# A list schedule that counts transfers by packets, the sample's bias copies moved to the prompt's attention, and four buffers for the u loads

## The chip, the cores and the metric

The kernel runs on one core of a Trainium2 chip. TensorE (PE) multiplies matrices; VectorE (DVE), ScalarE (ACT) and GpSimd (POOL) work elementwise and on rows; SyncE (SP) issues all transfers here, in the order of its queue (rows of SP in the profile are written SPq). Each engine works through its own instructions in their order, and waits where an operand is not there. The metric is the device time of one launch in microseconds, as the median of several runs.

## The reference

One encoder layer is applied with the same weights to a prompt of 512 tokens and a sample of 1024 tokens, each of width 1024:

```
h    = rmsnorm(x)
q_a,k_a,v_a,z_a, q_b,k_b,v_b,z_b, g_a,g_b = split(h @ w_in)
o_a  = neighbourhood_attention(rms(q_a), rms(k_a), v_a, rpb)   # 8 heads, 2-D window, bias
o_b  = window_gqa(rms(q_b), rms(k_b), v_b, t5 bias, sink)      # 8 heads, band of 3 blocks
A    = (o_a * silu(z_a)) @ w_o_a
B    = (o_b * silu(z_b)) @ w_o_b
y    = x + (sigmoid(g_a) * A + sigmoid(g_b) * B) @ w_out
```

All of it is float32. The kernel keeps that accuracy by splitting each operand into a high and a low part (`whi`/`wlo`, `hh`/`hl`, `fh`/`fl`) and adding three products, so one product is three matmuls (L1286, L1287, L1288 in the dense part, and L761 three times in the projections).

## The kernel before, in words

The program does four phases in turn: the prompt's attention (to about 200 us of the profile), the prompt's dense phase (gates z and g, output projections, `w_out`; from 222 to 405 us TensorE does nothing but this work), the sample's attention (405 to about 790 us) and the sample's dense phase (to the end).

Nobody writes the engines' order by hand. The kernel describes operations with `f.op` and `f.dma`: a choice of engines with an assumed duration each, a priority, what buffers it takes new, uses, or waits for. `Flow.run` then plays a simulation: at each moment it gives each engine the ready operation of the best priority whose buffers are free, adds the assumed duration, and emits the instruction. The order in which instructions were emitted is the order in which each engine does them on the chip. So an assumed duration is never waited for on the chip; it only decides what stands ahead of what. A transfer occupies the simulated SP for its issue time; its length is put on one simulated transfer resource (`dma_free`), and its data counts as landed 950 ns after that.

An attention phase goes in groups of heads. `att_weights` loads weights `w` (384 KB each, two buffers) with SP, ScalarE copies the high part `whi` (L602), POOL or VectorE subtracts for `wlo` (L607); projections (L761) into `p`; squares and row sums, POOL's `rs_v` (L792) and `rs_r` (L799) give the norm's factor, VectorE scales `qk` (L816), TensorE transposes it (L861) and ScalarE and VectorE copy `kt`, `qt`. Scores (L934), maximum, exps (L978, ScalarE), the reciprocal `rs` (L1002), the scaling `sb` (L1010), TensorE's transposes of `sb` (L1026), copies `pp` (L1032), the product with `v` (L1063), and the outputs `ot` to memory (`o_d`). Parts of the dense gates' work (matmuls L1286 to L1288 into bank `d`, with weights `fr` split into `fh` and `fl`) are put between as filling. `rstd` loads a tile of the sample (`xt`, 512 KB) and squares it (`junk`, L460) for the sample's norm during the prompt's attention.

The bias of the neighbourhood attention is prepared in memory: `expand` copies each head's table twice, shifted, into `rpb_x` (16 copies from memory to memory of 8 x 8 runs of 384 floats for each of prompt and sample), `raw` loads it (L682, L708), and POOL or VectorE adds the mask into `bias` (L695). For the sample the 16 copies are issued in the prompt's dense phase, released by the attention's last exps.

In the sample's dense phase the gated outputs `u` are kept in memory (`u_d`). For each of 8 blocks of columns and each half of the tokens, one `u` half (256 KB) is loaded into an `ot` buffer (two of them, L1552), split into `T` by ScalarE (L1168) and VectorE or POOL (L1173), and multiplied with `w_out`'s split weights. `post_z` (around L1417) multiplies an attention output with silu(z), for branch B through a strided view.

Of the kernel before, what the change touches and what calls it, by code (L numbers as in the profile page):

```python
# [10 lines left out]
F32 = mybir.dt.float32  # L11
F32R = mybir.dt.float32r
AF = mybir.ActivationFunctionType
ALU = mybir.AluOpType
# [26 lines left out]
P = 128  # L41
# [5 lines left out]
NT_P, NT_S = 512, 1024  # L47
# [93 lines left out]
class Flow:  # L141
# [43 lines left out]
        self.ops.append(o)  # L185
        return o

    def dma(self, emit, nbytes, prio, **kw):
        return self.op((("sp", 470),), lambda e: emit(), prio, lag=nbytes / 360, **kw)

    def stage(self, prio, close=(), open=(), make=()):

# [14 lines left out]
    def run(self):  # L207
# [58 lines left out]
        now, done, dma_free = 0, 0, 0  # L266
        while done < len(self.ops):
            for e in ready:
                while free_at[e] <= now:
                    skipped, got = [], None  # L270
                    while ready[e]:
                        item = heapq.heappop(ready[e])
                        o = item[2]
                        if o.eng is not None:
                            continue
                        ns = dict(o.choice)[e]
                        if all(room(v, n) for v, n in o.new) and not any(locked(v, e) or v.held and not v.t for v in o.vals) and not barred(o, e) and all(
                            e2 == e or backlog(e2, item) + n2 >= now + ns - BIAS.get((e, e2), 0) for e2, n2 in o.choice
                        ):
                            got = o  # L280
                            break
                        skipped.append(item)
                    for item in skipped:
                        heapq.heappush(ready[e], item)
                    if got is None:
                        break
                    got.eng = e
                    if got.port and e in ("dve", "pool"):
                        port = (e, now + ns)
                    for v, _ in got.new:  # L290
                        rota.setdefault(v.key, []).append(v)
                        v.make()
                    for v in got.vals:
                        v.lock = (e, now + ns)
                    got.emit(e)
                    free_at[e] = now + ns
                    at(now + ns, 0, got)
                    if got.lag:
                        dma_free = max(dma_free, now + ns + 650) + got.lag
                        at(dma_free + 950, 2, got)  # L300
            if not events:
                if DEBUG:
                    for e in ready:
                        for p, k, o in sorted(ready[e])[:4]:
                            print(e, p, k, [(v.tag, room(v, n), v.turn, len(rota.get(v.key, ()))) for v, n in o.new], [v.tag for v in o.vals])
                raise RuntimeError("no operation can go on")
            now = events[0][0]
            while events and events[0][0] == now:
                _, _, kind, o = heapq.heappop(events)
                if kind == 1:  # L310
                    o.left -= 1
                    if not o.left:
                        push(o)
                    continue
                if kind == 4:
                    continue
                if kind == 3:
                    o.free = True
                    continue
                if kind == 0 and o.lag:  # L320
                    continue
                done += 1
                for v in o.vals:
                    v.left -= 1
                    if not v.left:
                        at(now + self.LAG.get((o.eng, v.first), 100), 3, v)
                for x in o.outs:
                    lags = [self.LAG.get((o.eng, e), 100) for e, _ in x.choice]
                    at(now + min(lags), 1, x)
# [25 lines left out]
def encoder_kernel(  # L355
# [93 lines left out]
    def rstd(pool, x, t, prio, load_prio, bufs, after=(), load_after=(), out=None):  # L449

        val = lambda shape, dt, tag, n: f.value(pool, shape, dt, tag, n)
        xt = val([P, D], F32, "xt", bufs)
        junk = val([P, D], mybir.dt.bfloat16, "junk", 1)
        ss, v = (val([P, 1], F32, "n" + n, bufs) for n in "sv")
        r = out or val([P, 1], F32, "nr", bufs)
        rv = lambda: r.t[:, t : t + 1] if out else r.t
        f.dma(lambda: nc.sync.dma_start(xt.t, x[t * P : (t + 1) * P, :]), 524288, load_prio, new=[xt], after=load_after)
        f.op(
            (("act", ACT_(D) + 93),),
            lambda e: act.activation(junk.t, xt.t, AF.Square, accum_out=ss.t), prio, new=[junk, ss], use=[xt], after=after,  # L460
        )
        f.op(
            (("pool", 164),),
            lambda e: nc.gpsimd.tensor_scalar(v.t, ss.t, 1.0 / D, EPS, op0=ALU.mult, op1=ALU.add),
            prio, new=[v], use=[ss],
        )
        f.op(
            (("pool", 464),), lambda e: nc.gpsimd.tensor_tensor(rv(), v.t, mhalf[:, :1], op=ALU.pow),
            prio, use=[v], **({"into": [r]} if out and t else {"new": [r]}),
        )  # L470
        return xt, r
# [78 lines left out]
    def norm_tile_t(pool, x_t, rb, hh, hl, t, prio, load_prio):  # L550

        tok = slice(t * P, (t + 1) * P)
        xt = f.value(pool, [P, D], F32, "xt", 2)
        f.dma(
            lambda: nc.sync.dma_start(
                xt.t.rearrange("p (k n) -> p k n", n=P), x_t[:, :, tok].rearrange("k p n -> p k n")
            ),
            524288, load_prio, new=[xt],
        )
        src = lambda k: ([], lambda: xt.t[:, k * P : (k + 1) * P])  # L560
        return xt, scaled_parts(xt, src, lambda: rb.t[:, tok], rb, hh, hl, t, 4, prio)

    def norm_pair(pool, x_t, rb, hh, hl, t, t_d, prio, load_prio):
# [10 lines left out]
        for j, in0, in1, dst in (  # L574
# [12 lines left out]
                    t_d[j, :, :, t * P : (t + 1) * P].rearrange("k p n -> p k n"),  # L587
                    h[dst]().rearrange("p (k n) -> p k n", n=P),
                ),
                262144, prio, after=[o], hold=[(x0, x1)[dst[1]]],  # L590
            )
        return {t: sum(e0, ()), t + n: sum(e1, ())}, stores

    def att_weights(src, n, prio, engs=("pool", "dve"), place=None, after=()):
# [2 lines left out]
        hi = f.value(wpool, [P, 768], F32R, "whi", 6)  # L597
        lo = f.value(wpool, [P, 768], F32R, "wlo", 6)
        sv = lambda: st.t[:, at : at + n]
        ld = f.dma(lambda: nc.sync.dma_start(sv(), src), 512 * n, prio, after=after, **({"new": [st]} if new else {"hold": [st]}))  # L600
        a = f.op(
            (("act", ACT_(n) + 40),), lambda e: act.activation(hi.t[:, :n], sv(), AF.Copy),  # L602
            prio, new=[hi], hold=[st], after=[ld],
# [10 lines left out]
    def expand_ops(geo, prios, after):  # L614
        for h in range(8):
            expanded[geo.nt, h] = [
                f.dma(lambda h=h, lo=lo: expand(geo, h, lo), 196608, prios[h], after=after[h // 2]) for lo in range(2)
            ]

    def setup(pool, prio, after):  # L620
# [27 lines left out]
    def attention_phase(geo, hh, hl, h_ops, mask_d, early, late):  # L648
# [24 lines left out]
        def tables(br, g, prio):  # L673
            nb_t = tile_([P, max(2 * at[-1], 4 * GW)], F32, "bias", 2)
            first = [nb_t]
            for i in range(2 if br == "A" else 4):
                raw = tile_([P, max(GW, 48 * geo.cw)], F32, "raw", RAW[nt])
                if br == "A":
# [1 line left out]
                    h = 2 * g + i  # L680
                    sp(
                        lambda raw=raw, h=h: nc.sync.dma_start(raw.t[:, :run], rpb_x[nt][h]),  # L682
                        run * 512, prio, new=[raw], after=expanded[nt, h],
                    )
                    for o, n, c0 in [(a + o, n, c0) for a, (_, runs) in zip(at, a_tables) for o, n, c0 in runs]:
                        nw = n // P * cw
# [15 lines left out]
                else:  # L702
# [6 lines left out]

                    for lo in range(2):  # L710
                        kw = {"new": [raw], "after": line_op} if lo == 0 else {"into": [raw]}
                        sp(lambda raw=raw, h=h, lo=lo: emit_load(raw, h, lo), 98304, prio, **kw)

                    def emit(e, i=i, raw=raw):
                        ov = nb_t.t[:, i * GW : (i + 1) * GW].rearrange("p (w c l) -> p w c l", w=3, l=2)
# [242 lines left out]
        def weigh(br, gi, g, block, sums, pss, sbs, nb_t, info, prio):  # L958
# [114 lines left out]
            if br == "A":  # L1073
# [16 lines left out]
                        dst = over(o_d[nt][0, g, 64 * i : 64 * i + 64], runs)  # L1090
                        nc.sync.dma_start(dst, ot.t[:64, 2 * i].rearrange("p (a b) -> p a b", b=64))

                stores[g, runs[0][0] // 512].append(sp(emit, 65536, prio, use=[ot]))
            else:
                for e in range(2):
                    dst = o_d[nt][e, 4 + 2 * g : 6 + 2 * g, :, runs[0][0] : runs[0][0] + P]
                    dst = dst.rearrange("c (i d) n -> d (c i) n", d=64)
                    o = sp(
                        lambda e=e, dst=dst: nc.sync.dma_start(dst, ot.t[e * 64 : e * 64 + 64]),
                        131072, prio, use=[ot],  # L1100
                    )
                    for c in (4 + 2 * g, 5 + 2 * g):
                        for n in range(nt // 512):
# [32 lines left out]
    def dense_phase(geo, hh, hl, h_ops, o_stores, exps_done, start, opened, tp, up, p0, p1, p2, x_t, y_t, classic, fill, after_gates=None, side=None):  # L1136
# [269 lines left out]
        def post_z(c, a, n, v, in_psum, prio):  # L1406
# [3 lines left out]
            for e, ot in enumerate(ots):  # L1410
                if c < 4:
                    src, dst = o_d[nt][e, c, :, a : a + n], lambda ot=ot: ot.t[:, :n]
                else:
                    src = o_d[nt][e, c].rearrange("p (i n) -> p i n", n=P)[:, :, a // nb : a // nb + m]
                    dst = lambda ot=ot: ot.t[:, :n].rearrange("p (i n) -> p i n", n=m)
                dma(
                    lambda dst=dst, src=src: nc.sync.dma_start(dst(), src), 512 * n, prio - 0.5, new=[ot],  # L1417
                    after=o_stores[c, a // nh],
                )
            ot, ov, sv = ots[0], lambda: ots[0].t[:, :n], lambda: sg.t[:, :n]  # L1420
            if len(ots) > 1:
# [1 line left out]
            if c < 4:  # L1423
                tt(sv, sv, ov, ALU.mult, n, prio, use=[sg, ot], into=[sg])
            else:
                gv = lambda: sv().rearrange("p (n i) -> p n i", n=m)
                tt(gv, gv, lambda: ov().rearrange("p (i n) -> p n i", n=m), ALU.mult, n, prio, use=[sg, ot], into=[sg])
            if short:
                split_u(c, a, n, sg, prio)
            else:  # L1430
# [116 lines left out]
        if not short:  # L1547
            for c in range(8):
                for n in halves:
                    st = tile_("ot", n_ot)  # L1550
                    dma(
                        lambda st=st, c=c, n=n: nc.sync.dma_start(st.t, u_d[c, :, half[n]]), 512 * nh, 10 + c // 4,  # L1552
                        new=[st], after=stores["u", c, n],
# [105 lines left out]
    setup(norm_p, -0.7, h_ops["p"][1][:1])  # L1659
    expand_ops(gp, [max(-1, (h // 2 - 1) * gp.nb) for h in range(8)], [h_ops["p"][t][:1] for t in (1, 3, 3, 3)])  # L1660
    o_p, exps, start = attention_phase(gp, *h_p, h_ops["p"], mask_p, early["p"], late["p"])
    rb = f.value(rb_pool, [P, NT_S], F32, "rb", 1)
    r_s = f.value(norm_p, [P, gs.nb], F32, "r_s", 1)
    for t in range(gs.nb):
# [20 lines left out]
            h_ops["s"].update(ends)  # L1685
            t_stores.append(stores)

    expand_ops(gs, [4 + h for h in range(8)], [[exps]] * 4)
    dense_phase(
        gp, *h_p, h_ops["p"], o_p, exps, start, opened, t_pool["p"], u_pool, d0["p"], d1["p"], d2["p"], xt_p, y_p, CLASSIC_P,  # L1690
        FILL_P, None, norm_sample,
# [95 lines left out]
```

## Time and profile before

| | |
|---|---|
| runs (us) | 1142.96, 1141.8, 1140.71; median 1141.8 |
| profiled execution | 1145.24 us, of which the span from first to last instruction is 1143.4 us |
| busy: PE, DVE, ACT, POOL | 1129.6, 858.3, 645.1, 319.4 us |
| granted TensorE clock, mean | 0.998 |
| packets moved | 129314, 168.26 MB |

Busy is what an engine spent in instructions, issue and waiting not counted. Engines overlap, so the columns are not added. A wait in brackets at a row's end is the idle time ahead of it and what ended it. In the chain of work each piece is followed back from the last instruction to what released it; a transfer there runs from its issue to its landing. The windows give what each engine was busy within a stretch of the span.

### The profile page before, as it was taken

How to read it: one execution, taken by the hardware profiler on the slowest of the kernel's cores; microseconds unless marked ns; L12 is line 12 of the kernel's file. 1: busy time of each engine (PE TensorE's matmuls, PEld its weight loads, DVE VectorE, ACT ScalarE, POOL GpSimd, SP SyncE). 2: the span in 40 equal slices, each digit the busy share in tenths (PEclk: the TensorE clock that was granted, in tenths of full speed). 3: DMA queues.
4: the chain of work that ended last, by engine and by line, in shares of the span. 5: the costliest groups of instructions: out<-in, count | busy, mean ns of one | idle time of the engine just before them, and what ended most of it. 6: DMA issues, size and time to landing. Idle time of an engine off the chain costs nothing.

```text
span 1143.4 us, 18577 instructions
## 1 busy us (share of the span) xinstructions
PE 1129.6 (99%) x6115; PEld 981.9 (86%) x6115; DVE 858.3 (75%) x1994; ACT 645.1 (56%) x1477; POOL 319.4 (28%) x420
## 2 busy tenths in 40 slices
PE   8999999999999999999999999999999999999998
PEld 7989988888888889999899988888888888788887
DVE  6868797587766467887868888886878665497984
ACT  6767997544433246574659888875633334342320
POOL 4644443000010044443514343420123221032110
PEclk9999999999999999999999999999999999999999
DMA  7844643488797422121313214135767545564072
GB/s 267 275 140 129 189 118 97 106 257 256 237 277 210 157 91 72 29 79 29 91 31 93 72 38 121 46 111 160 262 179 228 194 161 186 196 230 130 28 221 93
DMA packets 129314, 168.26 MB, mean 147 GB/s; under 512 B 28809, under 2 KB 67473, under 8 KB 129218
## 3 DMA queue, kind: packets, MB, share of 16 engines
q1 hardware_dynamic: 129218, 167.08, 47.9%
q8 instruction: 48, 0.79, 0.3%
q14 instruction: 48, 0.39, 0.1%
HBM read 128.22 MB, written 43.54 MB: 150 GB/s over the span
## 4 chain that ended last, share of the span: by engine, by line
PE 92%; DMA 3%; DVE 2%; ACT 1%; POOL 1%; issue 1%; SPq 0%; POOLq 0%; DVEq 0%; ACTq 0%
PE p L761 23%; PE x L1288 10%; PE x L1287 10%; PE x L1286 10%; PE x L1063 5%; PE x L1026 5%; PE x L934 5%; PE p L1287 4%; PE p L1286 4%; PE p L1288 4%; PE d L1286 4%; PE d L1288 4%; PE d L1287 4%; PE x L861 2%; DMA w<-in_w_att_dram 1%
## 5 line engine op out<-in xcount | busy, mean ns | idle before, releaser
L761 PE MATMUL p<-whi,hh 128*128 128x384 f32 x384 | 133.8, 349 | 0.0
L761 PE MATMUL p<-whi,hl 128*128 128x384 f32 x384 | 132.7, 345 | 0.0
L761 PE MATMUL p<-wlo,hh 128*128 128x384 f32 x384 | 132.3, 345 | 0.0
L978 ACT ACTIVATE sb<-sb,mx 128x384 f32<-128x384 f32 (+1 forms) x192 | 107.8, 566 | 24.1 <-DVE mx L969 23.7
L761 PE MATMUL p<-whi,hb 128*128 128x384 f32 x384 | 107.8, 346 | 0.0
L1168 ACT ACTIVATE whi<-raw 128x512 fp32r<-128x512 f32 (+1 forms) x124 | 73.8, 607 | 60.2 <-PE x L1287 29.5
L1287 PE MATMUL x<-T,whi 128*128 128x512 f32 x256 | 99.7, 390 | 0.2 <-DVE T L1173 0.2
L1286 PE MATMUL x<-T,whi 128*128 128x512 f32 x256 | 99.7, 389 | 0.0
L1288 PE MATMUL x<-T,wlo 128*128 128x512 f32 x256 | 99.6, 389 | 0.0
L1037 DVE TENSOR_TENSOR pp<-x,pp 128x512 fp32r<-128x512 f32 (+1 forms) x136 | 82.6, 638 | 20.8 <-ACT pp L1032 19.7
L1288 PE MATMUL x<-hh,wlo 128*128 128x512 f32 (+1 forms) x232 | 89.8, 387 | 0.0
L1287 PE MATMUL x<-hl,whi 128*128 128x512 f32 (+1 forms) x232 | 89.8, 387 | 0.0
L1286 PE MATMUL x<-hh,whi 128*128 128x512 f32 (+1 forms) x232 | 89.8, 387 | 0.0
L1173 POOL TENSOR_TENSOR wlo<-raw,whi 128x512 fp32r<-128x512 f32 (+1 forms) x27 | 35.6, 1323 | 182.7 <-ACT whi L1168 182.6
L1173 DVE TENSOR_TENSOR wlo<-raw,whi 128x512 fp32r<-128x512 f32 (+1 forms) x97 | 65.3, 680 | 25.8 <-ACT whi L1168 25.4
L1032 ACT ACTIVATE pp<-x 128x512 fp32r<-128x512 f32 (+1 forms) x136 | 71.0, 560 | 24.0 <-PE x L1026 22.8
L799 POOL TENSOR_TENSOR rs_r<-rs_v,mhalf 128x4 f32<-128x4 f32 (+1 forms) x72 | 79.6, 1106 | 5.7
L792 POOL TENSOR_SCALAR rs_v<-ss 128x4 f32<-128x4 f32 (+1 forms) x72 | 26.8, 373 | 182.3 <-DVE ss L785 179.6
L1063 PE MATMUL x<-pp,v 128*128 128x256 f32 (+1 forms) x368 | 76.7, 322 | 0.0
L761 PEld LDWEIGHTS p<-whi,hl 128*128 128x128 f32 x384 | 73.1, 190 | 1.3 <-issue 1.0
L761 PEld LDWEIGHTS p<-whi,hh 128*128 128x128 f32 x384 | 73.1, 190 | 1.1 <-issue 0.5
L761 PEld LDWEIGHTS p<-wlo,hh 128*128 128x128 f32 x384 | 73.0, 190 | 0.9 <-issue 0.5
(351 smaller groups left out, 3012.9 us busy)
## 6 DMA issues: line engine op xcount, KB each, us to landing
raw<-in_w_g_dram SPq DMA_DIRECT2D x84, 256.0 KB
w<-in_w_att_dram SPq DMA_DIRECT2D x46, 384.0 KB
ot<-o_d SPq DMA_DIRECT2D x36, 256.0 KB
g_d<-C SPq DMA_DIRECT2D x34, 256.0 KB
raw<-in_w_z_dram SPq DMA_DIRECT2D x32, 256.0 KB
raw<-in_w_out_dram SPq DMA_DIRECT2D x32, 256.0 KB
fr<-in_w_g_dram SPq DMA_DIRECT2D x28, 256.0 KB
C<-g_d SPq DMA_DIRECT2D x24, 256.0 KB
```

The lines of the kernel that those rows point to most:

```text
L761: pe.matmul(ps.t[:, :GW], part[u](k), mv.t[:, c], start=k == 0 and m == 0, stop=k == KC - 1 and m == 2,)
L799: lambda e: nc.gpsimd.tensor_tensor(r.t[:, :nn], rv.t[:, :nn], mhalf[:, :nn], op=ALU.pow),
L934: pe.matmul(pss[2 * pair + i].t[:, :width], q.t[rows, u, at : at + P], kv[:, tiles[0] : tiles[-1] + 1 : step], start=n == 0, stop=n == 2,)
L978: act.activation(sb.t[:, :width], sb.t[:, :width], AF.Exp, bias=mx.t[:, i : i + 1], scale=-1.0, accum_out=sm.t[:, i : i + 1],)
L1032: lambda e, pt=pt, pp=pp, nn=nn: act.activation(pp.t[:, 0, :nn], pt.t[:, :nn], AF.Copy),
L1037: lambda e, pt=pt, pp=pp, nn=nn: dve.tensor_tensor(pp.t[:, 1, :nn], pt.t[:, :nn], pp.t[:, 0, :nn].bitcast(F32), op=ALU.subtract),
L1063: pe.matmul(out(), v.t[:, vs], mv(), start=first, stop=last)
L1168: (("act", ACT_(n)),), lambda e: act.activation(hi(), src(), AF.Copy), prio,
L1173: lambda e: engines[e].tensor_tensor(lo(), src(), hi().bitcast(F32), op=ALU.subtract), prio,
L1286: pe.matmul(out, hi.t[:, cs], mh(), start=first and k == 0, stop=False, **more)
L1287: pe.matmul(out, hi.t[:, cs], ml(), start=False, stop=False, **more)
L1288: pe.matmul(out, lo.t[:, cs], mh(), start=False, stop=last and k == len(ws) - 1, **more)
```

## The change

Four things are changed.

1. `Flow.dma` takes a transfer's run of contiguous bytes and its issue time. Its length was nbytes / 360 ns; now it is nbytes / run packets of (9 + run / 26) ns on 16 engines. Issue was 470 ns for every transfer, now 430, and by kind 470 to 690 (640 per part for `o_d`). Data counts as landed 1050 instead of 950 ns after. Work is not added or removed by it; the simulated order of all engines is drawn anew.
2. `post_z`'s multiply through the strided view is counted as 890 columns long.
3. The u loads of the second half of the tokens go to a buffer `fr` (two, so far idle there), those of the first half stay in `ot` (two).
4. The sample's 16 `rpb_x` copies are released by steps of the prompt's attention (when its 9th, 11th, 13th and 15th step have begun), and no longer by its last exps.

```diff
-    def dma(self, emit, nbytes, prio, **kw):
-        return self.op((("sp", 470),), lambda e: emit(), prio, lag=nbytes / 360, **kw)
+    def dma(self, emit, nbytes, prio, run=2048, issue=430, **kw):
+
+        lag = nbytes / run * (9 + run / 26) / 16
+        return self.op((("sp", issue),), lambda e: emit(), prio, lag=lag, **kw)
...
                         dma_free = max(dma_free, now + ns + 650) + got.lag
-                        at(dma_free + 950, 2, got)
+                        at(dma_free + 1050, 2, got)
...
-        ld = f.dma(lambda: nc.sync.dma_start(sv(), src), 512 * n, prio, after=after, **({"new": [st]} if new else {"hold": [st]}))
+        ld = f.dma(lambda: nc.sync.dma_start(sv(), src), 512 * n, prio, 3072, after=after, **({"new": [st]} if new else {"hold": [st]}))
...
-                f.dma(lambda h=h, lo=lo: expand(geo, h, lo), 196608, prios[h], after=after[h // 2]) for lo in range(2)
+                f.dma(lambda h=h, lo=lo: expand(geo, h, lo), 196608, prios[h], 1536, 690, after=after[h // 2]) for lo in range(2)
...
-                tt(gv, gv, lambda: ov().rearrange("p (i n) -> p n i", n=m), ALU.mult, n, prio, use=[sg, ot], into=[sg])
+                tt(gv, gv, lambda: ov().rearrange("p (i n) -> p n i", n=m), ALU.mult, 890, prio, use=[sg, ot], into=[sg])
...
-                    st = tile_("ot", n_ot)
+                    st = f.value(wpool, [P, nh], F32, "fr", 2) if n else tile_("ot", n_ot)
...
+    expand_ops(gs, [9 + h for h in range(8)], [[f.begun[NT_P, 9 + 2 * i]] for i in range(4)])
...
-    expand_ops(gs, [4 + h for h in range(8)], [[exps]] * 4)
```

The changed kernel's line numbers are 2 higher than those of before in what follows. Three places show how the order moves: the weights of the prompt's group 3, the start of the sample's attention, and the u loads. Numbers behind a name (w_940) count the buffers' uses and differ between the two kernels.

ScalarE in the prompt's attention, at the weights of group 3 (`whi`) ahead of the exps of a group's scores; before:

```order
L602 ACTIVATE whi<-w_795 128x768
L806 ACTIVATE v<-p 128x2x64
L882 ACTIVATE kt<-x,gcol 128x128
L896 ACTIVATE qt<-x,gq 128x128
L780 ACTIVATE sq<-p 128x256
L806 ACTIVATE v<-p 128x2x64
L602 ACTIVATE whi<-w_940 128x768
L602 ACTIVATE whi<-w_957 128x768
L978 ACTIVATE sb,sm<-sb,mx 128x256 x4
```

and now:

```order
L604 ACTIVATE whi<-w_787 128x768
L782 ACTIVATE sq<-p 128x256
L808 ACTIVATE v<-p 128x2x64
L884 ACTIVATE kt<-x,gcol 128x128
L898 ACTIVATE qt<-x,gq 128x128
L604 ACTIVATE whi<-w_961 128x768
L604 ACTIVATE whi<-w_974 128x768
L884 ACTIVATE kt<-x,gcol 128x128
L898 ACTIVATE qt<-x,gq 128x128
L462 ACTIVATE junk,ns<-xt 128x1024
L980 ACTIVATE sb,sm<-sb,mx 128x256 x4
```

The pair of `whi` still stands ahead of the exps; the copies of another block's `kt` and `qt`, and the squares of a sample tile, have come between.

TensorE at the scores of these exps, before (L1286 to L1288 are fills; the first transposes of `sb`, L1026, come 20 projections, three fills, the two transposes at L861 and two more projections behind the scores):

```order
L1286 MATMUL d<-hh,fh 128x512
L1287 MATMUL d<-hl,fh 128x512
L1288 MATMUL d<-hh,fl 128x512
L761 MATMUL p<-whi,hh 128x384
L761 MATMUL p<-wlo,hh 128x384
L761 MATMUL p<-whi,hl 128x384
L761 MATMUL p<-whi,hh 128x384
L934 MATMUL x<-kt,qt 128x256 x12
```

and now:

```order
L1290 MATMUL d<-hh,fl 128x512
L863 MATMUL x<-ident,qk 128x128 x2
L763 MATMUL p<-whi,hh 128x384
L763 MATMUL p<-wlo,hh 128x384
L763 MATMUL p<-whi,hl 128x384
```

with nine more projections in the same rotation behind these, and then

```order
L936 MATMUL x<-kt,qt 128x256 x12
L863 MATMUL x<-ident,qk 128x128 x2
L763 MATMUL p<-whi,hh 128x384
L763 MATMUL p<-wlo,hh 128x384
L763 MATMUL p<-whi,hl 128x384
```

Between the last fill and the scores stood 4 projections; now it is two transposes and 12 projections. Six fills and 12 projections (11 before) lie ahead of that, back to the previous pair's second `whi`. Behind the scores stand two transposes, 20 projections, another pair's 12 scores and one projection until the first transposes of `sb`.

SP at the same place, before:

```order
L1087 DMA o_d_79<-ot__901 64x2x128
L600 DMA w_940<-in_w_att_dram 128x768
L600 DMA w_957<-in_w_att_dram 128x768
L1091 DMA o_d_79<-ot__921 64x2x64 x2
L457 DMA xt<-in_x_s_dram 128x1024
L600 DMA w_1019<-in_w_att_dram 128x768
L600 DMA w_1052<-in_w_att_dram 128x768
```

and now, with the first four of the moved copies:

```order
L602 DMA w_961<-in_w_att_dram 128x768
L602 DMA w_974<-in_w_att_dram 128x768
L459 DMA xt<-in_x_s_dram 128x1024
L602 DMA w_1040<-in_w_att_dram 128x768
L602 DMA w_1054<-in_w_att_dram 128x768
L414 DMA rpb_x_76<-in_rpb_dram 8x8x384 x4
```

The sample tile `xt` goes directly behind the pair of weights, and copies stand between later weights: eight rows on, three more of them are next ahead of the load of w_1360.

POOL at the start of the sample's attention, where `bias` waits for the mask, before:

```order
L792 TENSOR_SCALAR rs_v<-ss 128x4
L799 TENSOR_TENSOR rs_r<-rs_v,mhalf 128x4
L792 TENSOR_SCALAR rs_v<-ss 128x4
L695 TENSOR_TENSOR bias<-mask,raw 128x24x8
L799 TENSOR_TENSOR rs_r<-rs_v,mhalf 128x4
L695 TENSOR_TENSOR bias<-mask,raw 128x16x8
L695 TENSOR_TENSOR bias<-mask,raw 128x24x8
```

and now:

```order
L794 TENSOR_SCALAR rs_v<-ss 128x4
L801 TENSOR_TENSOR rs_r<-rs_v,mhalf 128x4
L697 TENSOR_TENSOR bias<-mask,raw 128x24x8 x2
L794 TENSOR_SCALAR rs_v<-ss 128x4
L801 TENSOR_TENSOR rs_r<-rs_v,mhalf 128x4
L794 TENSOR_SCALAR rs_v<-ss 128x4
L801 TENSOR_TENSOR rs_r<-rs_v,mhalf 128x4
```

The second `rs_v` and `rs_r` now stand behind two bias steps.

SP at the u loads of the sample's dense phase, before, one piece out of the middle:

```order
L1552 DMA ot<-u_d_93 128x512
L1250 DMA raw<-in_w_g_dram 128x512
L1552 DMA ot<-u_d_93 128x512
L1578 DMA U<-g_d_94 128x512
L1552 DMA ot<-u_d_93 128x512
```

and now:

```order
L1554 DMA ot<-u_d_93 128x512 x2
L1252 DMA raw<-in_w_g_dram 128x512
L1554 DMA fr<-u_d_93 128x512 x2
L1580 DMA U<-g_d_94 128x512
L1554 DMA ot<-u_d_93 128x512
```

Four u loads now stand close together where three stood singly; two more `fr` loads stand 41 and 47 rows ahead of the first `ot` pair.

More of the change, by code (lines that the diff above doesn't have):

```diff
@@ L456, in rstd @@
         rv = lambda: r.t[:, t : t + 1] if out else r.t
-        f.dma(lambda: nc.sync.dma_start(xt.t, x[t * P : (t + 1) * P, :]), 524288, load_prio, new=[xt], after=load_after)
+        f.dma(lambda: nc.sync.dma_start(xt.t, x[t * P : (t + 1) * P, :]), 524288, load_prio, 4096, 470, new=[xt], after=load_after)
         f.op(
@@ L557, in norm_tile_t @@
             ),
-            524288, load_prio, new=[xt],
+            524288, load_prio, 512, 610, new=[xt],
         )
@@ L589, in norm_pair @@
                 ),
-                262144, prio, after=[o], hold=[(x0, x1)[dst[1]]],
+                262144, prio, 512, after=[o], hold=[(x0, x1)[dst[1]]],
             )
@@ L682, in tables @@
                         lambda raw=raw, h=h: nc.sync.dma_start(raw.t[:, :run], rpb_x[nt][h]),
-                        run * 512, prio, new=[raw], after=expanded[nt, h],
+                        run * 512, prio, 4 * run, new=[raw], after=expanded[nt, h],
                     )
@@ L711, in tables @@
                         kw = {"new": [raw], "after": line_op} if lo == 0 else {"into": [raw]}
-                        sp(lambda raw=raw, h=h, lo=lo: emit_load(raw, h, lo), 98304, prio, **kw)
+                        sp(lambda raw=raw, h=h, lo=lo: emit_load(raw, h, lo), 98304, prio, 1536, 560, **kw)
                     def emit(e, i=i, raw=raw):
@@ L1091, in emit @@
                         nc.sync.dma_start(dst, ot.t[:64, 2 * i].rearrange("p (a b) -> p a b", b=64))
-                stores[g, runs[0][0] // 512].append(sp(emit, 65536, prio, use=[ot]))
+                stores[g, runs[0][0] // 512].append(sp(emit, 65536, prio, 512 // len(runs), 640 * len(runs), use=[ot]))
             else:
@@ L1099, in weigh @@
                         lambda e=e, dst=dst: nc.sync.dma_start(dst, ot.t[e * 64 : e * 64 + 64]),
-                        131072, prio, use=[ot],
+                        131072, prio, 512, 640, use=[ot],
                     )
@@ L1416, in post_z @@
                 dma(
-                    lambda dst=dst, src=src: nc.sync.dma_start(dst(), src), 512 * n, prio - 0.5, new=[ot],
-                    after=o_stores[c, a // nh],
+                    lambda dst=dst, src=src: nc.sync.dma_start(dst(), src), 512 * n, prio - 0.5,
+                    *((2048,) if c < 4 else (4 * m, 570)), new=[ot], after=o_stores[c, a // nh],
                 )
```

## The prediction

> **What bounds the kernel now.** I read the page's busy shares first, then TensorE's waits, then windows over the span, then the chain of work and the engines' timelines at the few places where TensorE stood. The shares, and TensorE's idle time by what it waited for (us in total, times, longest):
>
> ```profile
> PE 1129.6 (99%) x6115; PEld 981.9 (86%) x6115; DVE 858.3 (75%) x1994; ACT 645.1 (56%) x1477; POOL 319.4 (28%) x420
> ...
> PE x L1644 <- DMA rb<-in_norm_row_dram: 4.6, 1, 4.6
> PE x L861 <- DVE qk L816: 3.1, 5, 1.0
> PE x L1026 <- DVE sb L1010: 2.3, 2, 2.0
> PE d L1286 <- ACT fc L1498: 0.2, 1, 0.2
> PE x L1287 <- DVE T L1173: 0.2, 1, 0.2
> ```
>
> TensorE does the same matmuls after the change, so only its idle time and its clock can move. The 4.6 us at the start are the first load, which nothing here touches. That leaves 3.1 + 2.3 + 0.2 + 0.2 = 5.8 us, in nine waits. Windows (us, PE busy, PEld, DVE, ACT, POOL, TensorE clock, DMA share, GB/s) put them in place:
>
> ```profile
> 76.00:222.00 146.00, 146.00 (x914) 130.22 (x913) 116.92 (x338) 115.16 (x289) 52.09 (x86) 1.00 0.44 124
> 222.00:405.00 183.00, 183.00 (x819) 152.83 (x818) 119.69 (x223) 76.33 (x129) 6.66 (x6) 1.00 0.76 231
> 405.00:425.00 20.00, 18.34 (x111) 16.70 (x109) 12.30 (x42) 7.71 (x25) 8.46 (x13) 1.00 0.21 66
> 425.00:552.00 127.00, 126.77 (x845) 120.00 (x846) 103.33 (x304) 79.82 (x220) 54.16 (x78) 1.00 0.19 54
> 552.00:556.00 4.00, 3.00 (x23) 2.21 (x22) 2.94 (x9) 1.10 (x3) 3.85 (x3) 1.00 0.50 130
> 973.00:977.00 4.00, 3.63 (x15) 2.31 (x14) 1.39 (x2) 1.79 (x3) 0.00 (x0) 1.00 0.92 319
> ...
> 71.00:75.00 4.00, 3.86 (x15) 3.64 (x16) 3.17 (x10) 3.17 (x9) 3.25 (x7) 0.57 0.52 164
> ```
>
> Two stretches of 146 and 183 us have no idle time at all. The last row is the one place with a slow clock: 4 us at 0.57 lose 4 × 0.43 = 1.7 us. So everything the change could give back is 5.8 + 1.7 = 7.5 us of 1143.4, and half of it sits at one place.
>
> **Place 1: prompt's attention, 69 us.** The chain (start, us, what), ScalarE's and SP's timelines, and TensorE's:
>
> ```profile
> 61.69 6.46 DMA w<-in_w_att_dram
> 68.93 1.58 ACT sb L978 x6
> ...
> 59.11 0.85 ACT L602 ACTIVATE whi<-w 128x768 fp32r<-128x768 f32 x1
> ...
> 63.74 0.85 ACT L602 ACTIVATE whi<-w 128x768 fp32r<-128x768 f32 x1 [1.93 <-DMA w<-in_w_att_dram]
> 68.18 0.85 ACT L602 ACTIVATE whi<-w 128x768 fp32r<-128x768 f32 x1 [3.59 <-DMA w<-in_w_att_dram]
> 71.32 1.05 ACT L460 ACTIVATE junk<-xt 128x1024 bf16<-128x1024 f32 x1
> ...
> 60.50 1.52 SPq L600 DMA_DIRECT2D w<-in_w_att_dram  x2
> 63.48 0.55 SPq L457 DMA_DIRECT2D xt<-in_x_s_dram  x1
> ...
> 63.28 0.97 PE L934 MATMUL x<-kt,qt 64*128 64x256 f32 x12
> 71.14 1.17 PE L1026 MATMUL x<-ident,sb 128*128 128x128 f32 x4 [1.96 <-DVE sb L1010]
> ```
>
> SP issues two weight loads from 60.50. The first is there at 63.74, 3.24 us later; the second takes 6.46 us. ScalarE works in order, so the exps (L978), whose scores were done at 64.3, stand behind that load's `whi` until 68.93. TensorE runs out of projections and idles 1.96 us, then runs slow: price 1.96 + 1.7 = 3.7 us.
>
> Now the changed order. The same pair of `whi` (w_961, w_974) stands ahead of the exps, but TensorE's rows put the scores later: between the previous pair's second `whi` and the scores stood 4.17 us of matmuls (59.11 to 63.28), and now there are 24 projections, 6 fills, 2 transposes. At the pitches of this undisturbed piece of chain
>
> ```profile
> 495.44 0.23 PE d L1286
> 500.06 0.37 PE x L861 x2
> 500.43 4.19 PE p L761 x24
> ```
>
> that is 4.19 + 6 × 0.23 + 0.37 = 5.9 us, 1.8 more. Behind the scores the cover is as long as before: 20 projections, 3 fills and 2 transposes then, 20 projections, 12 scores and 2 transposes now, about 4.9 us each. The loads thus have 1.8 us more, where 1.96 was missing: even a load as late as this one would leave 0.2 us, and a punctual one nothing. New is `junk` (L462, it waits for a 512 KB `xt` load) ahead of the exps. Punctual, it costs nothing: 1.52 + 0.55 of issue, 3.72 of landing (row below) and 1.05 of `junk` let the exps begin 6.84 us after the loads' issue; before, no idle time would have come up to 66.97, that is 6.47 after issue, now 1.8 later, 8.27.
>
> ```profile
> 50.18 3.72 DMA xt<-in_x_s_dram
> ```
>
> The bounds are 0 (a load is late again and `junk` carries it) and −3.7. I take −3.4, near the full amount, since both loads must be punctual only within 1.4 us. [...]
>
> **Place 2: start of the sample's attention, 405 to 425 us**, 1.66 us idle in the window: TensorE's two waits there, the third one's row, and what is behind the second and third.
>
> ```profile
> 406.39 0.44 PE L861 MATMUL x<-ident,qk 128*128 128x128 f32 x2 [0.48 <-DVE qk L816]
> 411.38 0.44 PE L861 MATMUL x<-ident,qk 128*128 128x128 f32 x2 [0.88 <-DVE qk L816]
> PE x L1026 <- DVE sb L1010: 0.3, 1, 0.3
> ...
> 409.13 0.71 POOL L695 TENSOR_TENSOR bias<-mask,raw 128x192 f32<-128x192 f32 x1 [2.07 <-DMA mask<-in_mask_s_dram]
> 421.34 1.28 ACT L978 ACT_TABLE_LOAD   x1
> ```
>
> POOL's second `rs_r`, on which the second wait hangs, stands behind a bias step that waits for the mask. After the change it stands behind two (+1.0 us, to 412.4), but TensorE gets 4 projections and 3 fills more ahead of its transposes: 4 × 0.175 + 3 × 0.23 = 1.4 us. Idle 0.88 − 0.4 = 0.5. The first wait has one projection less in front (+0.17). The table load of 1.28 us, which ends in the 0.30, moves ahead of the scores, where TensorE has work: −0.30. Sum −0.4 + 0.17 − 0.30 = −0.53; bounds −1.66 (all goes) and +1.0 (POOL's further step in full).
>
> **Place 3, 522 us** (the 0.23 in the window 425 to 552): three bias steps waiting for a `raw` copy stand ahead of POOL's `rs_v`; after, fewer do. −0.2, bounds −0.23 and +0.3. **Place 4, 552 us** (1.00): an operation of VectorE takes 1.85 us beside a long pair of POOL's `wlo`,
>
> ```profile
> 550.78 3.81 POOL L607 TENSOR_TENSOR wlo<-w,whi 128x768 fp32r<-128x768 f32 x2 [0.26 <-ACT whi L602]
> 551.06 1.85 DVE ot__7028 L1080
> ```
>
> and the order there is row for row the old one: 0.
>
> **Place 5, 973 to 977 us** (0.37 idle in the window): the four u buffers.
>
> ```profile
> 970.51 4.92 DMA ot<-u_d
> 975.46 0.64 ACT T L1168
> 976.12 0.70 DVE T L1173
> ```
>
> A u load is issued when one of two `ot` buffers comes free, and its split is TensorE's next operand. With `fr` for every other half, two `fr` loads stand 41 and 47 SP rows ahead of the first `ot` pair, and later loads go in pairs; a u load still comes late only if four are used up. −0.4; bounds 0 and −0.4. The other u loads wait at ScalarE alone, under a busy TensorE.
>
> **The sixteen copies.** Each occupies SP about 0.67 us (five in 3.35 below); removed from the prompt's dense phase, they free SP where TensorE had 183.00 busy of 183.00: 0. In the attention SP has gaps too, but weight loads are queued behind the copies: three ahead of w_1360 are 2.0 us.
>
> ```profile
> 219.29 3.35 SPq L412 DMA_DIRECT2D rpb_x<-in_rpb_dram  x5
> ```
>
> At place 1 only 1.26 of the 3.22 us of lateness were covered without idling (3.22 − 1.96). But w_1360 is the first of a pair, as at 63.74, where a load came 1.93 us after ScalarE was free and TensorE had no idle. I take 0, with bounds 0 and 3.7 for each pair that comes late. The transfers of 96 KB fall in a stretch at 124 GB/s (76 to 222), so bandwidth is there. [...]
>
> **The new numbers.** Transfers' assumed lengths come out near the old (a weight load 1092 against 1017 ns), issue 470 against 430, landing 950 against 1050. They cost nothing themselves but draw the order anew over 419 us of attention outside places 1, 2 and 4. There the old order has 0.23 + 0.23 of idle time; I take +0.5 for the new (bounds 0 and +2.0, two waits as long as place 4's). The multiply at 890 ns only chooses between VectorE and POOL in the dense phase, with 183.00 of 183.00: 0. The last 628 matmul rows are the same.
>
> **Sum:** −3.4 − 0.5 − 0.2 − 0.4 + 0.5 = −4.0 us, on the profiled 1145.24 (1143.4 of span and 1.8 around it): 1141.2. That execution was 3.4 us above the median of 1141.8, so the forecast is 1141.8 − 4.0 = 1137.8, taken as 1138.
>
> **Rivals.** *Place 1 gives nothing* (25%): either the late load belongs to the profiled execution, which is 3.4 us above the median, about that place's 3.7, or the new `junk` holds the exps when its `xt` is as late as that load was: 6.84 + 3.2 = 10.0 against 8.27 allowed gives 1.8 us idle and the slow clock again. For it speaks the coincidence of the two numbers; against it, that three runs spread only 2.2 us. Then −0.6: 1141.2, no change. *The copies hold back weight loads* (13%): the exps stand behind a `whi` whose load is over 1.3 us late; two such pairs cost 7.4, together −4.0 + 7.4: 1145.2, slower. *The clock is not lost for idling that short* (7%): were the 0.57 something that stays, place 1 is worth 2.0 less 0.3: 1139.5, at the edge. The forecast has 55%.
>
> **Range and chances.** The low end takes the whole ceiling at places 1, 2 and 5 without new waits, 1141.8 − 3.7 − 1.7 − 0.2 − 0.4 = 1135.8, less 0.8 for the runs' spread: 1135. The high end takes in the first rival and part of the second: 1144. For the forecast alone it is 1135.5 to 1140. What a measurement here tells from no change is 0.2%, 2.3 us. Faster than 1139.5: most of the forecast's 55 and half of the clock's 7, 57%; within: 29%; slower than 1144.1: 14%.
>
> **What would show it.** At place 1: no TensorE idle before the first transposes of group 3, clock 1.00 throughout. At the second QK transposes of the sample's attention about 0.5 us. No TensorE wait on a u load. Sum of the waits for qk and sb near 3 us instead of 5.4. Wrong would make it: a `whi` waiting over 3 us for its load with exps behind, a clock below 1.00 anywhere, `raw` loads behind the sixteen copies, or waits over 2 us at places that had none.

## The result, and the profile after

The changed kernel takes 1144.33 us (median of 20 runs, 1142.64 to 1146.76), the kernel before 1141.3 (20 runs, 1140.17 to 1145.72). The ratio is 1.0022, with a 95% interval of 1.0013 to 1.003: slower by about 3 us, a small loss but clear of the noise, where 1138 us, faster than before, was forecast. The profiled execution of the changed kernel took 1146.76 us, 2.4 above its median and the longest of its 20.

TensorE's share, and its waits after the change:

```profile
PE 1130.2 (99%) x6115; PEld 980.0 (86%) x6115; DVE 857.7 (75%) x1979; ACT 654.7 (57%) x1483; POOL 317.0 (28%) x429
...
PE x L1646 <- DMA rb<-in_norm_row_dram: 4.6, 1, 4.6
PE x L863 <- DVE qk L818: 2.4, 4, 1.0
PE x L534 <- DVE xt L522: 1.0, 1, 1.0
PE d L1288 <- ACT fc L1500: 0.9, 2, 0.7
PE x L1289 <- POOL T L1175: 0.8, 1, 0.8
PE x L1289 <- DVE T L1175: 0.5, 2, 0.2
PE x L534 <- PE p L763: 0.3, 1, 0.3
```

The wait of 2.3 us for `sb` is gone, the waits for `qk` are less, and waits of 1.0 us and less of five kinds, 3.5 us together, stand in their place. Without the first load the waits add up to 5.9 us, before to 5.8: the loss is not to be read from this list alone. Windows of the changed kernel at the places that the prediction speaks of, and at two it doesn't (148 and 973 to 985 us):

```profile
68.00:76.00 8.00, 8.00 (x62) 7.21 (x61) 6.45 (x26) 5.68 (x17) 2.20 (x6) 1.00 0.65 204
148.00:150.00 2.00, 1.32 (x7) 0.75 (x6) 2.00 (x5) 1.63 (x6) 0.00 (x0) 1.00 0.59 136
405.00:425.00 20.00, 19.38 (x122) 18.11 (x120) 12.95 (x46) 8.89 (x27) 10.94 (x18) 1.00 0.24 74
973.00:985.00 12.00, 10.73 (x43) 7.62 (x44) 7.50 (x11) 4.90 (x8) 1.48 (x2) 1.00 0.90 334
```

At place 1 TensorE is busy throughout at full clock. Of the 20 us at place 2 it now idles 0.62 (one wait, for the first `qk`), before 1.66. At 148 us it waits for `fc`, and in the u loads' stretch it idles 1.27 us; in the same window of before it idled 0.37:

```profile
973.00:985.00 12.00, 11.63 (x50) 8.87 (x49) 5.45 (x8) 4.70 (x8) 0.97 (x1) 1.00 0.79 285
```

Place 1 on ScalarE and SP in the changed kernel: both `whi` run at once when TensorE's order lets them, `junk` follows without a wait, and so do the exps.

```profile
67.54 1.74 ACT L604 ACTIVATE whi<-w 128x768 fp32r<-128x768 f32 x2
...
70.91 1.06 ACT L462 ACTIVATE junk<-xt 128x1024 bf16<-128x1024 f32 x1
...
63.98 1.21 SPq L602 DMA_DIRECT2D w<-in_w_att_dram  x2
65.28 0.38 SPq L459 DMA_DIRECT2D xt<-in_x_s_dram  x1
```

So the places came out much as drawn, and still the kernel is slower. The experiments ask which part does it.

### The profile page after: what moved, and what is told of

Read it like the earlier page. It is cut to its first block, busy times and chain, and to the rows that moved or that the text cites. A ratio compares the mean times of both kernels' runs of the same rounds, so it can differ in the third digit from the quotient of the medians.

```text
span 1144.7 us, 18573 instructions
## 1 busy us (share of the span) xinstructions
PE 1130.2 (99%) x6115; PEld 980.0 (86%) x6115; DVE 857.7 (75%) x1979; ACT 654.7 (57%) x1483; POOL 317.0 (28%) x429
## 5 line engine op out<-in xcount | busy, mean ns | idle before, releaser
L1288 PE MATMUL x<-T,whi 128*128 128x512 f32 x256 | 99.9, 390 | 0.0
L1175 DVE TENSOR_TENSOR wlo<-raw,whi 128x512 fp32r<-128x512 f32 (+1 forms) x105 | 70.1, 670 | 32.0 <-ACT whi L1170 25.2
L1288 PE MATMUL x<-hh,whi 128*128 128x512 f32 (+1 forms) x232 | 89.8, 387 | 0.0
L801 POOL TENSOR_TENSOR rs_r<-rs_v,mhalf 128x4 f32<-128x4 f32 (+1 forms) x72 | 82.6, 1147 | 5.5
L763 PEld LDWEIGHTS p<-whi,hb 128*128 128x128 f32 x384 | 69.0, 188 | 2.9 <-issue 1.0
L1028 PE MATMUL x<-ident,sb 128*128 128x128 f32 x496 | 70.8, 273 | 0.2
```

Of the source, the lines that this page charges most:

```text
L763: pe.matmul(ps.t[:, :GW], part[u](k), mv.t[:, c], start=k == 0 and m == 0, stop=k == KC - 1 and m == 2,)
L801: lambda e: nc.gpsimd.tensor_tensor(r.t[:, :nn], rv.t[:, :nn], mhalf[:, :nn], op=ALU.pow),
L1028: pe.transpose(pt.t[:, u * P : (u + 1) * P], sbs[i].t[:, c * P : (c + 1) * P], ident)
L1175: lambda e: engines[e].tensor_tensor(lo(), src(), hi().bitcast(F32), op=ALU.subtract), prio,
L1288: pe.matmul(out, hi.t[:, cs], mh(), start=first and k == 0, stop=False, **more)
```

## The experiments

Each ran beside the kernel before on the same chip; the medians of before were 1141.36 (first four), 1141.36 (next four) and 1141.22 (last four). Theory R: part 1, by drawing the order anew, makes the loss, whatever its numbers. Rivals: the u loads make it; the copies in front of weight loads make it.

**Part 1 alone** (the two lines of `Flow.dma` and all its arguments; u, copies and multiply as before).

```diff
+        lag = nbytes / run * (9 + run / 26) / 16
...
+                        at(dma_free + 1050, 2, got)
```

> Only the transfers' lengths, issue times and landing (part 1) are changed against before; the u loads stay in ot, the copies in the prompt's dense phase, the multiply at its old count. If the redrawn order of the attention phases makes the loss (in the two profiles: +1.0 us at the start, +1.2 at 40 to 56 us, +1.2 at 98 to 102, +0.9 at 149): 1143 to 1144.5, slower than before by 2 to 3 us. If the u loads or the copies make it: 1140.5 to 1142, like before.

1145.39 us, 6 runs; ratio 1.0036 (1.0022 to 1.005). Part 1 alone costs the whole loss and one more us, 0.9 above the top of what was expected of it.

**The u loads alone.**

```diff
-                    st = tile_("ot", n_ot)
+                    st = f.value(wpool, [P, nh], F32, "fr", 2) if n else tile_("ot", n_ot)
```

> Only the u loads' second halves go to fr; everything ahead of the sample's dense phase stands as before. If the u loads make the loss (the profile of after loses 3.2 us at 973 to 985 us, before 1.1): 1143 to 1143.5, and TensorE waits for a T whose fr load is late. If the redrawn order makes it: 1140.8 to 1141.8. The prompt's attention is before's row for row: if the late weight load at 69 us is a usual event, its 2 us wait and clock of 0.57 show in this profile too; if it belonged to that one execution, it is not there.

1141.83 us, 12 runs; ratio 1.0005 (0.9996 to 1.0014), so not clearly another time. Its profile has the wait, though. Windows of 965 to 985 us, first with four buffers, then before; then, of four buffers, the chain's load and the rows of ScalarE and TensorE behind it:

```profile
965.00:985.00 20.00, 18.48 (x76) 13.65 (x75) 12.65 (x21) 10.89 (x19) 1.29 (x1) 1.00 0.86 300
...
965.00:985.00 20.00, 19.63 (x86) 15.49 (x85) 10.79 (x16) 9.91 (x17) 3.58 (x3) 1.00 0.85 288
...
972.10 7.74 DMA fr<-u_d
...
979.87 0.63 ACT L1168 ACTIVATE T<-fr 128x512 fp32r<-128x512 f32 x1 [3.05 <-DMA fr<-u_d]
980.55 0.50 PE L1286 MATMUL x<-T,whi 128*128 128x512 f32 x1 [0.69 <-ACT T L1168]
```

1.52 us are idle instead of 0.37. With four buffers the planner also has TensorE need all u halves earlier: the last `T` is made at 981 us, and in before several are still made after 985. Its last u load is issued at 974 us; before issues its last five from 985.9 on. The transfers were already 0.85 busy there, and a load of the last pair takes 7.74 us where the late one of before took 4.92.

**The copies alone.**

```diff
+    expand_ops(gs, [9 + h for h in range(8)], [[f.begun[NT_P, 9 + 2 * i]] for i in range(4)])
...
-    expand_ops(gs, [4 + h for h in range(8)], [[exps]] * 4)
```

> Only the sixteen rpb_x copies are moved to the prompt's attention; TensorE's order is before's but for a few rows. If copies in front of weight loads make the loss: 1143 to 1145, with TensorE idle before L1026 or L861 and a whi waiting for its load. If the redrawn order or the u loads make it: 1140.5 to 1142.

1140.64 us, 12 runs; ratio 0.9992 (0.9982 to 1.0003). TensorE's order is the same as before's row for row. If the copies hold back weight loads, it costs nothing that the time shows; if they do anything it is to help. This is the fastest of all kernels here, but not clearly faster than before.

**All but u.** The changed kernel with u in `ot`.

> The changed kernel with all u loads back in ot. If the u loads make 2 us of the loss: 1142 to 1142.5. If the redrawn order makes it: 1143.7 to 1144.5, as after.

1143.76 us, 12 runs; ratio 1.0016 (1.0007 to 1.0026). Still slower than before; u is worth 0.6 us of after's 3.0, about the 0.5 of u alone; neither difference is clear of noise by itself.

**All but part 1.** The changed kernel with lengths, issue and landing of before.

```diff
-        lag = nbytes / run * (9 + run / 26) / 16
+        lag, issue = nbytes / 360, 470
```

> The changed kernel with the old lengths, issue times and landing of transfers: copies, u loads and multiply as after, the attention's order as before but for the copies. If the redrawn order alone makes the loss, this is 0.5 (u) and -0.7 (copies) from before: 1140.5 to 1142. If the parts only hurt together: 1143 to 1144.5.

1141.53 us, 12 runs; ratio 0.9999 (0.999 to 1.0007). With before's numbers the other three parts together change nothing. The loss is part 1's.

**All but the multiply.**

> The changed kernel with the strided multiply at its old count; TensorE's order is after's row for row. Expected 1143.8 to 1144.8, like after; its profile is a second draw of after's order: if 149 us (0.7 us wait for fc) and the u loads at 973 to 985 us (about 2 us more than before) belong to the order they are there again; if the 1.0 us at the start and the 1.1 us at 98 to 102 us belonged to the one execution they are not.

1144.88 us, 7 runs; ratio 1.0032 (1.0021 to 1.0043): like after, as expected of a kernel with after's TensorE order. Its profile has the wait for `fc` and the u loads' loss again, but not the wait of 1.0 us at the start, which stood in one of two executions of this order, and at 98 us it loses 0.4 us where after lost 1.1.

**Landing alone, and 430 alone.** One number of before is changed in each.

```diff
-                        at(dma_free + 950, 2, got)
+                        at(dma_free + 1050, 2, got)
```

> Before with one number changed: data counts as landed 1050 instead of 950 ns after. It changes about two fifths of TensorE's order too. If any new drawing of the order costs some us against the one of before: 1142.5 to 1145. If it is what the new lengths and issue times put where: 1140.5 to 1142.

> Before with one number changed: issue 430 instead of 470 ns for every transfer, lengths and landing as before. Another drawing of the order, over half of TensorE's rows. If any new drawing costs: 1142.5 to 1145; if not: 1140.5 to 1142.

Landing: 1147.47 us, 6 runs; ratio 1.0049 (1.0035 to 1.0063). 430: 1147.07 us, 6 runs; ratio 1.005 (1.0032 to 1.0067). Either number by itself costs more than the whole change. In the 430 kernel the prediction's first rival is to be seen at work, in ScalarE's and TensorE's rows and the window behind:

```profile
73.32 1.06 ACT L460 ACTIVATE junk<-xt 128x1024 bf16<-128x1024 f32 x1 [5.47 <-DMA xt<-in_x_s_dram]
76.59 0.81 PE L1026 MATMUL x<-ident,sb 128*128 128x128 f32 x4 [2.37 <-DVE sb L1010]
...
75.00:80.00 5.00, 3.41 (x16) 3.16 (x17) 3.80 (x12) 3.92 (x14) 1.59 (x3) 0.79 0.00 0
```

`junk` waits 5.5 us for its sample tile, the exps wait behind it, TensorE idles 2.4 us and then runs slow.

**Landing by 1 ns, and by −10 ns.** 950 becomes 951, or 940.

> Before with the landing counted as 951 instead of 950 ns, nothing else. It redraws TensorE's rows 125 to 820 alone, the prompt's attention; the rest stands as before. If before's order is a favourable draw among many, this is slower by 1 to 4 us (1142.5 to 1145.5) and the loss lies before 200 us; if a redrawing as such costs nothing, 1140.8 to 1142.

> The same with 940 ns: another draw of TensorE's rows 125 to 818. Favourable-draw theory: 1142.5 to 1145.5, loss before 200 us. Else 1140.8 to 1142.

951: 1145.7 us, 10 runs; ratio 1.0038 (1.0022 to 1.0053). 940: 1147.25 us, 6 runs; ratio 1.0043 (1.0024 to 1.0061). One nanosecond in the planner costs 4.5 us, and ten the other way 6.0, so it isn't the direction in which the number is changed. The place was expected wrong in part: besides the prompt's attention, both lose at 358 us, in the dense phase, where TensorE's rows are before's. There the chain through the two `ot` buffers (a gate's load, its product, the sum `C`, the split `hh`) runs behind TensorE; its last gate load is issued at 349.9 us with 951, at 343.5 in the kernel with u alone, while TensorE is only 2.6 us later. Why the chain falls so far behind was not followed further up. TensorE's wait in the 951 kernel and the window after it:

```profile
358.95 0.50 PE L1286 MATMUL x<-hh,whi 128*128 128x512 f32 x1 [1.71 <-ACT hh L1168]
...
360.00:365.00 5.00, 5.00 (x16) 3.95 (x15) 1.51 (x3) 1.05 (x2) 0.00 (x0) 0.66 0.61 211
```

**Lengths alone.** Issue 470 and landing 950 stay.

> Of part 1 only the transfers' lengths by packets, issue 470 and landing 950 as before. If the new numbers are each harmless and a draw decides: slower by 2 to 6 us, as the landing and the 430 alone. If the lengths are what is right about the change: 1139 to 1141.5.

1152.15 us, 6 runs; ratio 1.0086 (1.006 to 1.0111), the slowest. The lengths by packets, the part that is meant to be right about the chip, give the worst order of all.

**Part 1 alone, a second profile.**

> The same kernel as the one with part 1 alone, for a second profile: four of its six executions had a mean clock of 0.998 or 0.999 and took 1145 to 1146.2, the profiled one 1.000 and 1141.96. Both theories of the order expect a place in the prompt's attention, before 200 us, with 2 us or more of idle time behind a weight or sample load and about 4 us at half clock after it; a wait elsewhere would be a third.

1145.43 us, one run. The expected kind of wait isn't there: no load is behind it. Both executions of this kernel idle most at one place, 144 to 149 us. The transpose at L1670 reads `r_s`, which POOL takes 1.84 us to make, with `es` close behind it (the view names `es`); then ScalarE is late with `fc`. TensorE's two waits, and the windows around them, of the first execution (1141.96 us) and of the second:

```profile
145.98 0.27 PE L1670 MATMUL x<-ident,r_s 128*8 128x128 f32 x1 [1.40 <-POOL es L996]
147.65 0.50 PE L1288 MATMUL d<-hh,fh 128*128 128x512 f32 x1 [0.69 <-ACT fc L1500]
...
141.85:145.27 3.42, 2.74 (x15) 2.42 (x15) 3.42 (x12) 3.42 (x9) 3.17 (x4) 1.00 0.55 137
145.27:148.68 3.41, 2.01 (x9) 1.35 (x9) 1.42 (x4) 1.71 (x6) 0.69 (x2) 1.00 0.68 216
148.68:152.09 3.41, 3.41 (x21) 3.14 (x20) 2.83 (x9) 3.36 (x11) 2.54 (x4) 1.00 0.53 160
...
147.21 0.27 PE L1670 MATMUL x<-ident,r_s 128*8 128x128 f32 x1 [1.40 <-POOL es L996]
148.88 0.50 PE L1288 MATMUL d<-hh,fh 128*128 128x512 f32 x1 [0.69 <-ACT fc L1500]
...
145.88:149.29 3.41, 1.39 (x6) 0.87 (x7) 1.50 (x4) 1.70 (x6) 1.31 (x2) 1.00 0.75 254
149.29:152.71 3.42, 3.42 (x12) 2.83 (x11) 2.27 (x5) 2.12 (x10) 1.55 (x4) 0.50 0.55 188
```

The idle times are equal to the hundredth, but only the second execution pays the slow clock behind them. The windows are cut at the steps of 3.41 us in which these traces' clock moves (last section), and they show why. In the first execution a step ends within the first wait, so that 0.68 us of idle time fall in one step and 1.40 in the next, and the clock stays. In the second both waits fall in one step, 2.02 us of its 3.41, and the next step runs at 0.50. Four of six timed executions had a mean clock of 0.998 or 0.999 and took 1145 to 1146.2 us; the two at 1.000 took 1142 and 1143.5. So where a fixed wait of 2.1 us falls among the steps decides whether about 1.5 us more are lost.

## Why the prediction was wrong

To compare orders, I took TensorE's start-to-start times less what each matmul takes in an undisturbed stretch (0.174, 0.227, 0.117 and 0.109 us for outputs of 384, 512, 256 and 128), and summed the rest by the same amount of matmul work. The pitches are typical ones, so a few tenths mean little. Lost us by stretch, in single executions:

| stretch (us of before) | before | u alone | copies alone | all but part 1 | after | all but multiply |
|---|---|---|---|---|---|---|
| 14 to 67 | 2.5 | 2.8 | 2.6 | 2.8 | 3.7 | 2.9 |
| 67 to 78 (place 1) | 3.9 | 0.1 | 0.2 | 1.9 | 0.3 | 0.5 |
| 78 to 138 | 1.2 | 1.1 | 1.2 | 1.1 | 2.0 | 1.6 |
| 138 to 152 (`fc`) | 0.3 | 0.3 | 0.3 | 0.3 | 1.2 | 1.2 |
| 404 to 453 (place 2) | 3.2 | 2.7 | 1.9 | 2.9 | 1.5 | 1.2 |
| 972 to 1005 (u loads) | 1.1 | 3.1 | 0.8 | 2.3 | 3.2 | 3.1 |

The first four kernels have before's TensorE order up to 404 us, the last two after's.

- **Place 1, −3.4: the term that failed first.** The mechanism was right, and after the change the loads are punctual enough, as worked out. But the price was that of one execution, and the prediction took it off the median of 1141.8, which didn't hold it. In two of four executions with that order the second load of the pair came late (its `whi` waited 3.59 us in before and 3.15 in all but part 1, against 1.29 with u alone and 1.48 with the copies alone), and of these two only the one I read lost the clock too: they lost 3.9 and 1.9 us, the others 0.1 and 0.2. Of 64 timed executions of before beside these experiments, none had a mean clock below 1.000; the profiled one had 0.998. The prediction saw that the profiled execution stood 3.4 us above the median, about this place's price, and gave that rival 25%. But the rival's own time was 1141.2, no change; the other 3.1 us up to the measured 1144.33 need the next term.
- **New waits of the redrawn order, +0.5: mis-sized.** It was taken from the idle time that the old order still had, and bounded at +2.0. Kernels with seven other orders measured +3.0 (after), +4.0, +4.5, +5.7, +6.0, +6.1 and +10.9 us (those of after and of part 1 alone part only at 125 us). The old order's few waits are no measure of what an order costs; it is the best of eight.
- **Place 2, −0.53: right in sign, more in size.** The stretch lost 2.7 on average with before's order and 1.4 with after's: −1.3. The second QK transposes came out without a wait where 0.5 was expected. **Place 3, −0.2:** the wait is gone. **Place 4, 0:** the 1.0 us are there again.
- **Place 5, −0.4: wrong in sign in the profiles.** The stretch gained 2.0 us of loss with u alone; in the times +0.5 (u alone, within its interval of none) and +0.6 (after against all but u). Two buffers had spread the loads; four let them bunch where the transfers were 0.85 busy.
- **Copies, 0:** right; measured −0.7, within its interval of none. The rival with held-back weight loads fell: such delay as there may be costs nothing that the time shows.
- **The multiply, 0:** TensorE's order is the same with and without.

What after has against a typical execution of before is then +0.9 for `fc`, about +2 for the u loads (a part is the order's: 1.9 with u in `ot` and after's order, against 0.8 and 1.1), −1.3 at place 2 and −0.2 at place 3: about +1.4. The rest of the +3 would by the table lie in the stretches 14 to 67 and 78 to 138 us, which together lose 5.7 and 4.5 us in two executions of after's order and 3.7 to 3.9 in four of before's; which waits make it was not found. What makes before's order hold better than the others was not found; that it was picked among many fits, but no run shows it.

## What to carry to other kernels

Where a planner's numbers set the order, a changed number is a new draw of the whole order, and being meant as truer to the chip did not make it faster: the lengths by packets alone cost 10.9 us here, and 1 ns 4.5. Compare a new model with several draws (the same model a few ns off) before it is called better or worse, and after a good draw expect a new one to be worse, as all seven were here. Before the largest wait of one profiled execution is counted as a gain, see that execution's time against the median and take a second profile: what stands in some profiles only is an event with a chance, not a cost of every run.

## What the runs showed of the hardware

In these traces TensorE's clock falls for one step of 3.41 us at a time, and the idle time within the step ahead tells in every one of them whether it falls. While TensorE has work, seven of the fourteen traces have one stretch at 0.50, each 3.41 us long, and the full speed recorded ahead of it lasts a whole number of such steps: 17 in before, 18 in 430, 40 in the second profile of part 1 alone, 102 in 951, in 940 and in landing alone, 104 in lengths alone. When each trace is cut into these steps, the step ahead of a slow one held 1.94 to 2.91 us of idle TensorE (1.94 in 951, 1.95 in before, 2.02 in the second profile of part 1 alone, 2.09 in 430, 2.91 in lengths alone, whose longest wait but for the first load is 2.9), and no other step held more than 1.65 (in lengths alone, where the clock held; 1.45 at place 1 in all but part 1, and 1.0 at place 4). A slow step costs half of it, 1.7 us: within it a dense matmul of 951 starts every 0.43 us, outside every 0.23. The limit between 1.65 and 1.94 us is these fourteen traces' alone.
